# Seven products for eight over the whole contraction, in the up-projection of a one-core decoder layer

## The chip, the cores and the metric

The kernel runs on one core of one Trainium2 chip. The metric is the device time of one launch in microseconds. Three runs of the kernel before took 2917.29, 2924.40 and 2925.81 us; their median is 2924.4.

## The reference

One decoder layer for 2048 prompt rows and 64 sample rows of width 1024: a mixer of two recurrent parts (RWKV-7 and HGRN2), then two post-norms around a squared-ReLU MLP. The change is in the MLP part alone:

```
h1 = layer_norm(ALPHA * h + mix, ln1_g, ln1_b)
up = square(relu(h1 @ w_up))                # 1024 -> 4096
ff = up @ w_down                            # 4096 -> 1024
h  = layer_norm(ALPHA * h1 + ff, ln2_g, ln2_b)
```

All is float32. The kernel splits each operand of a product into a high part and a low part (the difference) and takes three matmuls for one: high by high, high by low, low by high (`mm3`). So one 128-column step of a contraction is three matmuls.

## The kernel before

**Stages.** The mixer's instructions are ordered by a planner (`Sched`), which also plans the first rows of the MLP (`begin`, `enter`). From `rest` on (about 1430 us) the order is written out: each engine takes its instructions in the order in which the program emits them, and so does SyncE, which issues the transfers. The MLP goes through three blocks of rows: block 0 with 576 rows (`first`), blocks 1 and 2 with 768 each (`block`). TensorE is PE, weight loads PEld, VectorE DVE, ScalarE ACT, GpSimd POOL, SyncE SP.

**A unit of blocks 1 and 2.** `up(j)` makes two column tiles of `up`, j and j + 16, for 768 rows, which stand as two halves of 384. `down` then adds the products of the two tiles before with the rows of `w_down` to the accumulators `acc`: twelve steps of six matmuls with 512 columns, each in one of four banks, followed by an add on DVE. With the two column tiles, the two row halves and two halves of the contraction, a product of 2 x 2 by 2 x 2 parts can be made with seven products instead of eight, if sums of the operands are formed first (Strassen's scheme in Winograd's form). Before, this is done over the first half of the contraction (four of eight tiles of 128; `seven`, two tiles each); over the other half all four products are made directly (`direct`, four tiles each). The seven products go to four banks; copies and adds on ACT and DVE (`m1`, `m5`, `u2` in the tile `mt`) combine them. `done` makes relu, square and a high part on ACT and a low part on DVE, into `uh` and `ul`.

**Operands of a unit.** `w_up` comes as `raw` tiles of 1024 columns; sums are formed on DVE (`t12`, `t34`), and `split` makes high and low parts (ACT, then DVE) into four slots of 512 columns, `uph` and `upl`. Some slots are filled twice a unit, the second time within `up` (`s3`, `s4`). The rows of `w_down` are split as whole 1024-column tiles into a ring of three (`wdh`, `wdl`).

**Between blocks.** `enters` transposes the next block's rows (PE), forms their sums (`sums`) and splits them into `xo`, `xd` and `xs`. Its nine entries are taken one by one within the last two `down` passes. The finished block's norms (`layer_norm`: statistics, center, scale) are put into `later` step by step in the last pass; `step` takes one from there. `finish` is the last down-projection of block 2, four tiles at once.

Of the kernel before, what the change touches and what calls it, by code (L numbers as in the profile page):

```python
# [8 lines left out]
F32 = mybir.dt.float32  # L9
# [40 lines left out]
STEPS = 8  # L50
# [1623 lines left out]
def mlp_phase(ctx, tc, em, a, o, z, banks, sch):  # L1674
# [16 lines left out]
    def bank(nm):  # L1691
        b0, n = {"pd": (0, 4), "pu": (4, 4), "pt": (4, 4)}[nm]
        i = cnt.get(nm, 0)
        cnt[nm] = i + 1
        return fix["banks"][b0 + i % n]
# [8 lines left out]
    def begin(free):  # L1704
# [7 lines left out]
        lnp.extend(pool.tile([128, 1024], F32, name=f"lnp{i}") for i in range(4))  # L1712
        for i in range(4):
            src = a["lnp"][i:i + 1, :]
            em.dma(lnp[i], bass.AP(tensor=src.tensor, offset=src.offset, ap=[[0, 128], [1, 1024]]))
            yield now() + APART
# [3 lines left out]

        for x in "hl":
            fix["xd" + x] = pool.tile([128, 3072], F32R, name="xd" + x)
            fix["xo" + x] = pool.tile([128, 2304], F32R, name="xo" + x)
        slots.extend((pool.tile([128, 512], F32R, name=f"uph{i}"), pool.tile([128, 512], F32R, name=f"upl{i}")) for i in range(4))
        yield "go"
        for mi, (t0, mt) in enumerate(blocks[0]):
# [5 lines left out]
            if mi == 0:  # L1732
                ahead(1, 0)
                yield now() + APART
                ahead(2, 0)
                yield now() + APART
            sch.add(enter(mi, mt, sch.clk[SP] + DMA_TIME + 3000), 2)
            yield "go"
        ahead(2, 1)
        yield "go"  # L1740

    def enter(mi, mt, t):

        yield t
        for f in layer_norm(accs[0][mi], mt, 0):
            f()
            yield
        for g in range(2):
            ps = yield from PT.get()
            tr_in(0, mi, g, ps)  # L1750
            yield
            tr_out(0, mi, g, ps)
            PT.put(ps)
            yield "go"


    slots = []
    uses = []
    for f in range(0, NFT, 2):
        uses.append([("up", f, 2 * (f % 2))])  # L1760
        if f == NFT - 2:
            uses.append([("up", f + 1, 2)])
        if f:
            uses.append([("wd", f - 2, None), ("wd", f - 1, None)])
        if f < NFT - 2:
            uses.append([("up", f + 1, 2)])
    uses.append([("wd", NFT - 2, None), ("wd", NFT - 1, 2)])
    w = {"dma": 0, "split": 0, "use": 0}
    raws, splits = [], []

    def ahead(n_dma, n_split):
        while w["split"] < min(n_split, len(uses)):
            while w["dma"] <= w["split"]:
                fetch()
            u = uses[w["split"]]
            splits.append([halves(raw, at) for (_, f, at), raw in zip(u, raws.pop(0))])
            w["split"] += 1
        while w["dma"] < min(n_dma, len(uses)):
            fetch()

    def halves(raw, at=None):

        if at is not None:
            for i in range(2):
                split(slots[at + i], raw[:, 512 * i:512 * i + 512])
            return slots[at:at + 2]
        h = ring("wdh", 3, [128, 1024], F32R)
        l = ring("wdl", 3, [128, 1024], F32R)
        split((h, l), raw)
        return [(h[:, 512 * i:512 * i + 512], l[:, 512 * i:512 * i + 512]) for i in range(2)]  # L1790

    def split(hl, x):
        em.act(hl[0], x, AF.Copy)
        em.tt(hl[1], x, hl[0].bitcast(F32), OP.subtract)

    def fetch():
        raws.append([load(nm, f) for nm, f, _ in uses[w["dma"]]])
        w["dma"] += 1
# [6 lines left out]
    def use():  # L1805

        ahead(0, w["use"] + 1)
        w["use"] += 1
        return splits.pop(0)

    def prepare():

        ahead(w["use"] + 2, w["use"] + 1)
# [12 lines left out]
    def layer_norm(t, mt, gi, then=None):  # L1826
# [520 lines left out]
```

## Time and profile before

| | us |
|---|---|
| median of three runs | 2924.4 |
| the profiled execution | 2921.14 |
| its span, first to last instruction | 2919.4 |
| PE busy | 2837.4 (97%) |
| DVE busy | 1972.7 (68%) |
| ACT busy | 1158.8 (40%) |
| POOL busy | 432.1 (15%) |

Matmuls overlap: each is shown from its start to the end of its pipeline, so the time that one takes is read from the starts of two that follow one another. A timeline row gives the start, the duration, the engine, the line and the operation with the tiles it writes and reads; in brackets stands how long the engine was idle before it and who released it. Where several equal instructions follow each other, one row shows them with their count and the time from the first start to the last end. L97 is the line of the matmul helper, L112 that of ACT's, L156 that of the two-input operation on DVE or POOL.

### The profile page before, as it was taken

Reading aid. Unit: us, or ns where it says so; the run is one execution under the profiler, and the core shown is the slowest. Engines: PE = TensorE matmul, PEld = TensorE weight load, DVE = VectorE, ACT = ScalarE, POOL = GpSimd, SP = SyncE. Lnnn points to the kernel's source line nnn. Section 1 sums busy time; section 2 is a strip of 40 time slices with the busy share of each in tenths; the row PEclk is TensorE's granted clock in tenths of the full one; section 3 lists DMA queues with packets and bytes.
Section 4 is the critical chain, followed back from the end, with each engine's and each line's share of the span. In section 5 each row is a group of like instructions: output and inputs, shape, how many; then the busy total and the mean of one; then the engine's idle time right before and its main releaser. Section 6 shows DMA issues by size and latency. Waiting matters only on the chain.

```text
span 2919.4 us, 54442 instructions
## 1 busy us (share of the span) xinstructions
PE 2837.4 (97%) x22110; PEld 2480.9 (85%) x22110; DVE 1972.7 (68%) x3826; ACT 1158.8 (40%) x2465; POOL 432.1 (15%) x430
## 2 busy tenths in 40 slices
PE   8999999999999999899999999899999999999998
PEld 8988877778777777889988889799999989999997
DVE  5776757868687687854445664776677677666566
ACT  5455323443444335333333333443443344433442
POOL 4332111011110012335300010200000020000002
PEclk9999999999999999999999999999999999999999
DMA  7535444534353443448532222122121112211221
GB/s 272 194 104 199 153 132 138 172 103 141 103 160 116 124 131 120 135 133 276 183 104 98 85 80 85 61 87 105 59 84 61 58 66 73 102 64 58 72 74 58
DMA packets 173196, 337.32 MB, mean 116 GB/s; under 512 B 29712, under 2 KB 51472, under 8 KB 172944
## 3 DMA queue, kind: packets, MB, share of 16 engines
q1 hardware_dynamic: 172944, 333.83, 34.3%
q8 instruction: 173, 2.83, 0.4%
q14 instruction: 79, 0.65, 0.1%
HBM read 270.65 MB, written 63.11 MB: 114 GB/s over the span
## 4 chain that ended last, share of the span: by engine, by line
PE 80%; DVE 12%; ACT 3%; DMA 2%; issue 2%; POOL 1%; SPq 0%; POOLq 0%; DVEq 0%; ACTq 0%
PE bank L97 79%; PE bank L108 2%; DVE rhsb L156 1%; DVE xt L156 1%; DVE xt L1005 1%; DVE et L160 1%; DMA raww<-in_wout 1%; DVE rs L160 1%; DVE et L900 1%; DVE acc L156 1%; POOL wl L156 0%; DVE st L1848 0%; DVE bk L160 0%; DVE upl L156 0%; DVE xl L156 0%
## 5 line engine op out<-in xcount | busy, mean ns | idle before, releaser
L156 DVE TENSOR_TENSOR acc<-bank,acc 128x512 f32<-128x512 f32 (+1 forms) x532 | 358.7, 686 | 119.2 <-PE bank L97 117.5
L97 PE MATMUL bank<-wdh,uh 128*128 128x512 f32 (+1 forms) x1054 | 413.3, 392 | 6.7 <-DVE acc L156 5.1
L97 PE MATMUL bank<-wdl,uh 128*128 128x512 f32 (+1 forms) x1054 | 411.9, 391 | 0.8 <-DVE wdl L156 0.8
L97 PE MATMUL bank<-wdh,ul 128*128 128x512 f32 (+1 forms) x1054 | 411.8, 391 | 0.0
L97 PE MATMUL bank<-xh,wh 128*128 128x512 f32 (+1 forms) x1040 | 383.9, 369 | 10.9 <-ACT wh L112 7.8
L97 PE MATMUL bank<-xl,wh 128*128 128x512 f32 (+1 forms) x1040 | 380.2, 366 | 0.6 <-DVE xl L156 0.6
L97 PE MATMUL bank<-xh,wl 128*128 128x512 f32 (+1 forms) x1040 | 374.8, 367 | 0.9 <-POOL wl L156 0.8
L97 PE MATMUL bank<-wh,xh 128*128 128x256 f32 (+1 forms) x816 | 248.8, 305 | 8.5 <-DVE rs L160 8.5
L97 PE MATMUL bank<-xdh,upl 128*128 128x384 f32 (+1 forms) x768 | 247.8, 323 | 5.6 <-DVE upl L156 5.6
L97 PE MATMUL bank<-xdh,uph 128*128 128x384 f32 (+1 forms) x768 | 247.2, 322 | 0.0
L97 PE MATMUL bank<-xdl,uph 128*128 128x384 f32 (+1 forms) x768 | 247.2, 322 | 0.0
L97 PEld LDWEIGHTS bank<-wdh,uh 128*128 128x128 f32 (+1 forms) x1054 | 194.8, 185 | 51.3 <-DVE acc L156 6.0
L97 PE MATMUL bank<-wh,xl 128*128 128x256 f32 (+1 forms) x816 | 235.0, 288 | 3.0 <-POOL xl L156 3.0
L97 PE MATMUL bank<-wl,xh 128*128 128x256 f32 (+1 forms) x816 | 235.1, 288 | 1.8 <-POOL wl L156 1.8
L156 DVE TENSOR_TENSOR upl<-raw,uph 128x512 fp32r<-128x512 f32 (+1 forms) x262 | 161.4, 628 | 110.4 <-ACT uph L112 110.2
L97 PEld LDWEIGHTS bank<-wdh,ul 128*128 128x128 f32 (+1 forms) x1054 | 194.9, 185 | 45.4
L97 PEld LDWEIGHTS bank<-xh,wh 128*128 128x128 f32 x1040 | 197.6, 190 | 40.8 <-ACT wh L112 8.0
L97 PEld LDWEIGHTS bank<-wdl,uh 128*128 128x128 f32 (+1 forms) x1054 | 194.9, 185 | 43.9 <-DVE wdl L156 1.1
L97 PEld LDWEIGHTS bank<-xl,wh 128*128 128x128 f32 x1040 | 197.5, 190 | 29.5 <-issue 4.8
L97 PEld LDWEIGHTS bank<-xh,wl 128*128 128x128 f32 x1040 | 196.1, 190 | 29.1 <-issue 4.8
L112 ACT ACTIVATE uph<-raw 128x512 fp32r<-128x512 f32 (+1 forms) x262 | 141.6, 569 | 169.0 <-DVE raw L156 144.8
L156 POOL TENSOR_TENSOR wl<-raww,wh 128x512 fp32r<-128x512 f32 x120 | 161.6, 1352 | 278.6 <-ACT wh L112 246.7
(261 smaller groups left out, 5843.8 us busy)
## 6 DMA issues: line engine op xcount, KB each, us to landing
raw<-in_wup SPq DMA_DIRECT2D x96, 512.0 KB, 3.5
raw<-in_wdown SPq DMA_DIRECT2D x96, 512.0 KB, 3.5
wh<-h_w SPq DMA_DIRECT2D x156, 256.0 KB, 2.7
wl<-l_w SPq DMA_DIRECT2D x156, 256.0 KB, 2.9
raww<-in_wout SPq DMA_DIRECT2D x64, 256.0 KB, 3.0
raww<-in_win SPq DMA_DIRECT2D x52, 256.0 KB, 3.3
h_w<-wh SPq DMA_DIRECT2D x52, 256.0 KB, 2.8
l_w<-wl SPq DMA_DIRECT2D x52, 256.0 KB, 2.3
```

The lines of the kernel that those rows point to most:

```text
L97: self.nc.tensor.matmul(out, lhsT, rhs, start=start, stop=stop, skip_group_check=skip)
L108: self.nc.tensor.transpose(out, in_, ident)
L112: self.nc.scalar.activation(out, in_, func, **kw)
L156: (self.nc.vector if eng == DVE else self.nc.gpsimd).tensor_tensor(out, a, b, op=op)
L160: self.nc.vector.scalar_tensor_tensor(out, a, s, b, op0=op0, op1=op1)
L900: nc.vector.tensor_tensor_scan(L[:, c0:c0 + per], ones.to_broadcast([128, per]), sg[:, c0:c0 + per], 0.0, op0=OP.add, op1=OP.add)
L1005: nc.vector.transpose(out, in_)
```

## The change

`up(j)` makes seven products over the whole contraction, with four tiles of 128 each, and no direct ones. For this `enters` forms all sums over eight tiles (`rows`, then `sums`, which has its low parts of sums made by POOL), with twelve entries; the operands stand in `xo` and `xs` alone. The sums of `w_up` are over 512 columns (`one` to `seven`), two of the subtractions on POOL; seven operand slots are filled per unit, three of them within `up`. `up` takes three banks of the four in turn. The weights of `w_down` are split in half tiles of 512 into four fixed slots (`wslots`); `down` goes through all rows with the first half of the columns and then with the second. A block's last norms are appended to `later` after its last `down` pass, so that they run behind the next block's operands, in `up` and `down` of its first units; `down` takes a norm step at its steps 0, 4 and 8 (before at step 0 alone). Only two norm parameter rows are held, and loaded anew when the kind of norm changes (`norm_params`).

Of the functions in the diff below the added and the kept lines are shown; the removed ones stand in the kernel above.

```diff
+    def load_down(*fs):
+        for f in fs:
+            new["wd", f] = load("wd", f)
+
+    def split(hl, x, eng=DVE):
+        em.act(hl[0], x, AF.Copy)
+        em.tt(hl[1], x, hl[0].bitcast(F32), OP.subtract, eng=eng)
+
+    def split_up(f):
+        raw = new.pop(("up", f))
+        for i in range(2):
+            split(slots[2 * (f % 2) + i], raw[:, 512 * i:512 * i + 512])
+
+    def split_down(fs, hfs=(0, 1)):
+        for hf in hfs:
+            for i, f in enumerate(fs):
+                split(wslots[2 * hf + i], new["wd", f][:, 512 * hf:512 * hf + 512])
+
+    def norm_params(gi, i):
+        src = a["lnp"][2 * gi + i:2 * gi + i + 1, :]
+        em.dma(lnp[i], bass.AP(tensor=src.tensor, offset=src.offset, ap=[[0, 128], [1, 1024]]))
...
+            got = []
+
+            def rows(g, mi=mi, got=got):
+                for m in (mi, mi + 3):
+                    got.append(bank("pu"))
+                    tr_in(bi, m, g, got[-1])
+
+            def sums(mi=mi, got=got):
+                a11, a21, a12, a22 = got
+                cs = slice(mi * 128, mi * 128 + 128)
+                t1, t2, t3 = (fix["mt"][:, 512 * i:512 * i + 512] for i in range(3))
+
+                def put(nm, k0, x, eng=DVE):
+                    part(nm, k0, 384, cs, x.rearrange("p (k t) -> p k t", k=4), eng)
+
+                em.act(t3, a21, AF.Copy)
+                em.tt(t1, a22, t3, OP.add)
+                put("xs", 0, t1, POOL)
+                em.tt(t2, t1, a11, OP.subtract)
+                put("xs", 4, t2, POOL)
+                em.tt(t3, a11, t3, OP.subtract)
+                put("xs", 8, t3, POOL)
+                put("xo", 0, a11)
+                em.tt(t1, a12, t2, OP.subtract)
+                put("xs", 12, t1, POOL)
+                put("xo", 8, a22)
+                put("xo", 4, a12)
+
+            def scale(mi=mi):
+                for m in (mi, mi + 3):
+                    t = accs[bi % 2][m]
+                    em.act(t, t, AF.Copy, scale=ALPHA)
+
+            out += [lambda r=rows: r(0), lambda r=rows: r(1), sums, scale]
...
+    def down(bi, fs, tasks, last=False, todo=()):
 
         acc = accs[bi % 2]
+        n = 0
+        for hf in range(2):
+            for mi, (t0, mt) in enumerate(blocks[bi]):
                 ps = bank("pd")
+                partial(ps, mi, mt, fs, wslots[2 * hf:2 * hf + 2], True, True)
                 s = slice(512 * hf, 512 * hf + 512)
                 em.tt(acc[mi][0:mt, s], ps[0:mt], acc[mi][0:mt, s], OP.add)
+                if todo and n % 2 == 0:
                     todo.pop(0)()
+                for x in tasks.get(n, ()):
+                    x()
+                if n % 4 == 0 and not todo:
+                    step()
+                n += 1
         if last:
             while todo:
                 todo.pop(0)()
+            lns = []
+            for mi, (t0, mt) in enumerate(blocks[bi]):
+                def put(t0=t0, mt=mt, t=acc[mi]):
+                    em.dma(o["y"][t0:t0 + mt], t[0:mt])
+
+                lns.append(layer_norm(acc[mi], mt, put))
+            for i in range(len(lns) + 2):
                 for j in range(3):
+                    if 0 <= i - j < len(lns):
...
+    def last_two(bi, fs, gs):
+
+        todo = enters(bi + 1)
+        n = len(blocks[bi])
+        down(bi, fs, {n + 1: [lambda: split_down(gs, (0,))]}, todo=todo)
+        down(bi, gs, {0: [lambda: split_down(gs, (1,))], 2: [unit.one], 4: [unit.two], 6: [unit.three], 8: [unit.four]}, last=True, todo=todo)
...
+        def one(self):
             self.f, self.g = self.new
             split(slots[0], self.f[:, 0:512])
+            em.tt(self.f[:, 0:512], self.g[:, 0:512], self.f[:, 0:512], OP.subtract)
+
+        def two(self):
+            f, g = self.f, self.g
+            split(slots[1], f[:, 0:512])
+            em.tt(f[:, 0:512], g[:, 512:1024], f[:, 0:512], OP.subtract)
+            em.tt(g[:, 0:512], g[:, 512:1024], g[:, 0:512], OP.subtract, eng=POOL)
+
+        def three(self):
+            split(slots[2], self.f[:, 0:512])
+
+        def four(self):
+            split(slots[3], self.g[:, 512:1024])
+
+        def five(self):
+            split(slots[0], self.g[:, 0:512])
+
+        def six(self):
+            split(slots[1], self.f[:, 512:1024])
+            em.tt(self.f[:, 512:1024], self.f[:, 512:1024], self.f[:, 0:512], OP.subtract, eng=POOL)
+
+        def seven(self):
             split(slots[2], self.f[:, 512:1024])
...
+            y, x, d = (bank("pu")[:, 0:384] for _ in range(3))
+            m1, m5, u2 = (fix["mt"][:, 512 * i:512 * i + 384] for i in range(3))
+
+            def seven(ps, nm, k0, slot, first=False):
                 wh, wl = slots[slot]
                 for k in range(4):
                     ws = slice(128 * k, 128 * k + 128)
-                    mm3(ps, wh[:, ws], wl[:, ws], *xs("xd", k, t, 768), first and k == 0, last and k == 3, True)
+                    xs = [fix[nm + z].rearrange("p (k t) -> p k t", t=384)[:, k0 + k] for z in "hl"]
+                    mm3(ps, wh[:, ws], wl[:, ws], *xs, first and k == 0, k == 3, True)
 
...
+            seven(y, "xo", 0, 0, True)
             em.act(m1, y, AF.Copy)
+            unit.five()
+            seven(x, "xs", 0, 1, True)
             em.act(m5, x, AF.Copy)
+            unit.six()
             step()
+            seven(y, "xs", 4, 2)
             em.act(u2, y, AF.Copy)
+            unit.seven()
+            if j:
+                split_down((j - 1, j + 15), (0, 1) if j == 15 else (0,))
+            if j == 15:
+                load_down(f, g)
+            seven(x, "xs", 12, 3)
+            em.tt(u2, x, u2, OP.add)
             if j < 15:
                 unit.load()
+            done(u2, g, 0)
+            seven(y, "xs", 8, 0)
             em.tt(m5, y, m5, OP.add)
+            if 0 < j < 15:
+                split_down((j - 1, j + 15), (1,))
+            if j < 15:
+                load_down(f, g)
             if j == 15 and not end:
                 unit.load()
+            if not j:
+                unit.one()
+                unit.four()
+            done(m5, g, 384)
+            seven(d, "xo", 4, 1, True)
+            em.tt(m1, d, m1, OP.add)
+            if not j:
+                unit.two()
+            done(m1, f, 0)
+            if j == 15 and end:
+                late(3, f, 0)
+                late(0, f, 1)
+                late(1, g, 0)
+            seven(y, "xo", 8, 2)
+            if j == 15 and end:
+                late(2, g, 1)
+            if not j:
+                unit.three()
             c = ring("c", 2, [128, 384], F32)
             em.act(c, y, AF.Relu)
             squared(c, f, 384)
...
+                down(bi, (j - 1, j + 15), {2: [unit.one], 4: [unit.two], 6: [unit.three], 8: [unit.four]})
...
                     step(len(later))
+                    for i in range(2):
+                        norm_params(0, i)
                     next_rows(bi + 1)
...
         step(len(later))
...
+        if not end:
+            for i in range(2):
+                norm_params(1, i)
+            last_two(bi, (14, 30), (15, 31))
             return
...
+        ws = [wslots[0::2], wslots[1::2], [slots[3], slots[0]], [slots[1], slots[2]]]
+        finish(bi, (14, 30, 15, 31), ws)
```

## Rows read from the trace of the kernel before

**Rows 1.** The page: busy time, share of the span and instructions of each engine.

```profile
PE 2837.4 (97%) x22110; PEld 2480.9 (85%) x22110; DVE 1972.7 (68%) x3826; ACT 1158.8 (40%) x2465; POOL 432.1 (15%) x430
```

**Rows 2.** Windows (busy us per engine, PE's granted clock, DMA): block 0, block 1.

```profile
1500.00:1550.00 50.00, 50.00 (x293) 43.90 (x292) 24.70 (x38) 17.02 (x34) 0.00 (x0) 1.00 0.39 139
...
1905.00:2340.00 435.00, 435.00 (x2198) 396.20 (x2197) 291.75 (x489) 170.53 (x322) 5.53 (x14) 1.00 0.21 75
```

**Rows 3.** Timeline (start, duration, engine, operation) of PE, one unit of block 2.

```profile
2499.72 0.39 PE L97 MATMUL bank<-wdh,uh 128*128 128x512 f32 x1
...
2504.94 0.39 PE L97 MATMUL bank<-wdh,ul 128*128 128x512 f32 x1
...
2508.32 0.33 PE L97 MATMUL bank<-xdh,uph 128*128 128x384 f32 x1
...
2510.23 0.33 PE L97 MATMUL bank<-xdh,upl 128*128 128x384 f32 x1
```

**Rows 4.** Timeline of ACT in that unit; in brackets the idle time before.

```profile
2508.39 0.63 ACT L112 ACTIVATE uph<-raw 128x512 fp32r<-128x512 f32 x1 [0.43 <-PE bank L97]
...
2511.66 0.49 ACT L112 ACTIVATE mt<-bank 128x384 f32<-128x384 f32 x1 [2.63 <-PE bank L97]
2512.05 0.41 ACT L112 ACTIVATE uph<-raw 128x256 fp32r<-128x256 f32 x1
2512.35 1.07 ACT L112 ACTIVATE mt<-mt 128x384 f32<-128x384 f32 x2
2513.46 0.53 ACT L112 ACTIVATE uh<-mt 128x384 fp32r<-128x384 f32 x1
...
2522.77 1.14 ACT L112 ACTIVATE uph<-raw 128x512 fp32r<-128x512 f32 x2
```

**Rows 5.** Timeline of DVE in that unit.

```profile
2509.06 0.69 DVE L156 TENSOR_TENSOR upl<-raw,uph 128x512 fp32r<-128x512 f32 x1 [1.81 <-ACT uph L112]
...
2514.02 0.56 DVE L156 TENSOR_TENSOR ul<-mt,uh 128x384 fp32r<-128x384 f32 x1 [1.10 <-ACT uh L112]
...
2523.38 1.28 DVE L160 SCALAR_TENSOR_TENSOR acc<-acc,rsd,lnp 128x1024 f32<-128x1024 f32 x1
2524.57 1.28 DVE L156 TENSOR_TENSOR acc<-bank,acc 128x512 f32<-128x512 f32 x2
```

**Rows 6.** Groups by line and form of POOL: count, busy us, mean ns, idle time before.

```profile
L156 POOL TENSOR_TENSOR wl<-raww,wh 128x512 fp32r<-128x512 f32 x120 | 161.6, 1352 | 278.6 <-ACT wh L112 246.7 <-PE bank L97 14.0 <-DMA z<-rs 8.1
```

**Rows 7.** Timeline of POOL and of DVE near the end of the mixer.

```profile
1303.63 1.28 POOL L156 TENSOR_TENSOR wl<-raww,wh 128x512 fp32r<-128x512 f32 x1 [1.31 <-ACT wh L112]
...
1344.84 1.97 POOL L156 TENSOR_TENSOR wl<-raww,wh 128x512 fp32r<-128x512 f32 x1 [1.25 <-ACT wh L112]
...
1344.38 1.28 DVE L160 SCALAR_TENSOR_TENSOR acc<-acc,mv,lnp 128x1024 f32<-128x1024 f32 x1
```

**Rows 8.** PE's waits (us in total, times, longest) at the two block changes and the end.

```profile
PE bank L97 <- DVE acc L156: 2.3, 2, 1.4
...
PE bank L97 <- DVE upl L156: 4.1, 1, 4.1
PE bank L97 <- ACT uph L112: 0.7, 1, 0.7
...
PE bank L97 <- DVE acc L156: 2.9, 3, 1.1
PE bank L97 <- DVE upl L156: 1.5, 1, 1.5
...
PE bank L97 <- ACT wdh L112: 1.4, 1, 1.4
PE bank L97 <- DVE wdl L156: 0.8, 1, 0.8
```

**Rows 9.** Timeline of PE after its 4.1 us wait.

```profile
1867.26 0.52 PE L97 MATMUL bank<-xdh,uph 128*128 128x384 f32 x1
...
1871.42 0.52 PE L97 MATMUL bank<-xsl,uph 128*128 128x384 f32 x1
```

More of the change, by code (lines that the diff above doesn't have):

```diff
@@ L1751, in enter @@
             yield
-            tr_out(0, mi, g, ps)
+            part("xo", 4 * g, 576, slice(n, n + mt), ps.rearrange("p (k t) -> p k t", k=4)[:, :, 0:mt])
             PT.put(ps)
+            if g:
+                em.ts(tl[0:mt], tl[0:mt], ALPHA, None, OP.mult, eng=POOL)
             yield "go"
[L1757 to L1798, printed above, removed]
+    new, slots, wslots = {}, [], []
     def load(nm, f):
@@ L2015, in up, with next_up, even, odd @@
                 squared(c, f, c0)
-        todo = []
-        for f in range(0, NFT - 2, 2):
-            up(f)
+        def next_up(f):
+            new["up", f] = load("up", f)
+        def even(f):
             if f:
-                down(0, (f - 2, f - 1), use(), {2: [prepare]})
-            up(f + 1)
+                split_down((f - 2, f - 1))
+            else:
+                split_up(1)
+            if f == NFT - 2:
+                split_up(f + 1)
+                load_down(f, f + 1)
+                return
+            next_up(f + 2)
+            if not f:
+                load_down(0, 1)
+        def odd(f):
+            if f == NFT - 1:
+                unit.load()
+                return
+            split_up(f + 1)
+            next_up(f + 2)
+        for f in range(0, NFT, 2):
+            up(f, lambda: even(f))
+            if 0 < f < NFT - 2:
+                down(0, (f - 2, f - 1), {2: [lambda: split_up(f + 1), lambda: load_down(f, f + 1)]})
+            up(f + 1, lambda: odd(f + 1))
             if f == 8:
@@ L2132, in up @@
-            seven(y, "xs", 2, 1, 256)
+            seven(y, "xs", 4, 2)
             em.act(u2, y, AF.Copy)
-            unit.s4()
+            unit.seven()
[5 more added lines that the diff above has]
+            em.tt(u2, x, u2, OP.add)
             if j < 15:
                 unit.load()
-            done(m1, f, 0)
-            direct(e, 384, 3, first=True)
@@ L2139, in up @@
-            seven(y, "xs", 4, 0, 0)
+            done(u2, g, 0)
+            seven(y, "xs", 8, 0)
             em.tt(m5, y, m5, OP.add)
-            if j:
-                split_down(j - 1, 0)
-            em.tt(m5, e, m5, OP.add)
-            done(m5, g, 384)
-            seven(x, "xs", 6, 0, 256, last=False)
-            if j == 0:
-                unit.s1()
-                unit.t12()
-            direct(x, 0, 3)
-            em.tt(u2, x, u2, OP.add)
-            if j:
-                split_down(j - 1, 1)
```

216 lines of the change are left out of this document (41 added, 175 removed).

## The prediction

> **What bounds the kernel now.** The page's first part shows TensorE (PE) busy 97% of the span, VectorE (DVE) 68%, ScalarE (ACT) 40%, GpSimd (POOL) 15% [rows 1]. Then the stretches: in the middle of block 1 PE is busy for 435.00 of 435.00 us at full granted clock [rows 2], and the list of PE's waits there is empty. So a matmul removed there is time removed, as long as nothing else becomes late. Third, the timeline of one unit (one pass of `up` and one of `down`), engine by engine, because it has the durations and the order [rows 3 to 5]. Last, PE's waits at the block changes, the only places of the MLP where it waits: 2.3 us, 4.1 and 0.7 at the first, 2.9, 1.5 and again 0.7 at the second, 2.2 before the last down-projection [rows 8].
>
> **The matmuls removed.** A unit of blocks 1 and 2 makes two column tiles for 768 rows. Before: seven products over four contraction tiles (7 x 4 x 3 = 84 at full contraction, here half: 42) and four direct ones over the other four (4 x 4 x 3 = 48), 90 matmuls of 384 columns; after: 84. There are 2 x 16 units, so 192 go. Twelve such matmuls start in 2508.32 to 2510.23, 0.174 us apart, though each is shown as 0.33 long because they overlap [rows 3]; the pitch is the price: **-33.4 us**. The 72 matmuls of `down` stay (0.227 apart [rows 3]).
>
> **The chain inside a unit.** All that hid before now has a shorter unit and another order, so I laid the emitted order of `up` on the durations of the rows, us from the unit's first matmul. The method, tried on the old unit, gives its starts within 0.15 us, for instance the ACT chain at 2512.35 and the low part at 2514.06 (trace: 2512.35 and 2514.02 [rows 4, 5]). Durations: an ACT split of 512 columns 0.62, the next 0.52 later; a chain relu, square, copy 1.64; a DVE low part 0.69, the next 0.60 later; a 384-column DVE add 0.56, 0.47 [rows 4, 5]; a hand-over 0.04 (ACT ends 2509.02, DVE starts 2509.06). POOL's 512-column subtraction 1.29 [rows 7] (1.35 on average [rows 6]).
> Each product is 12 matmuls, 2.09 us; its result is there 0.16 after the next has begun.
> - 4.38: ACT copies the second product; 4.77 to 5.39 `six` splits; 5.43 to 6.12 DVE's low part; then `six` subtracts on POOL, 6.21 to 7.50.
> - `seven` splits what POOL wrote, and ACT stands in line for it: 7.53 to 8.15. Behind it come two splits of `split_down`, to 9.19. DVE's three low parts start at 8.19, 8.79, 9.39.
> - The add that makes u2 needs a product finished at 8.52, but is queued behind those on DVE: 9.99 to 10.55. ACT's three steps 10.59 to 12.23. DVE's low part of u2 at 12.26, and only then m5's add, 12.73 to 13.29, though its product was there at 10.61.
> - The seventh product writes the bank `y` that this add reads. PE could start it at 12.53 and waits until 13.34: **0.8 us**.
> Nothing gives it back: the next unit begins later by as much. It holds for passes 1 to 14 of both blocks, 28 x 0.8 = 22.4. In pass 15 all four splits stand ahead of u2's add (1.2 more): 2 x 2.0 = 4.0. In pass 1, which follows pass 0 with no `down` between, the second product takes the bank that pass 0's last relu still reads: 2 x 1.0 = 1.9. Together **+28.3**. Bounds: if ACT's `seven` did not have to wait for POOL, u2's add would start 0.65 earlier and the wait fall to 0.15 (8 us in all); with POOL at its mean 1.35 it is 0.05 longer a unit (30).
>
> **The norms on top.** After m5's add the four chains follow one another, ACT and DVE in turn: m1's add 15.5, the last relu 17.6, its low part 19.3, DVE free at 19.76. The first add of `down` then ends at 20.45; PE needs its bank for step 4 at 20.86. Slack 0.4; the old unit had a norm step ahead of its first add (2523.38, 2524.57 [rows 5]) and PE waited nowhere. A norm step at the end of `up` (center or scale 1.19 of DVE's time [rows 5], the statistics taken as the same) makes PE wait 0.85, the one at step 0 delays the next add and adds 0.45: 1.3 in 12 units (passes 1 to 3 of both blocks, where the norms of the block before now are, and 7 to 12 of block 1), 15.8; a third norm step at step 8 adds 0.8 in five of these, 4.1; small delays in passes 1 and 2 make 1.6. **+21.5**, between 0 (if the slack is 1.3 larger) and 27.
>
> **The block changes.** DVE no longer does norms there (they stood in the last `down` pass), but one call of `sums` holds it for 7 us: seven operations of 0.6, and waits for ACT's copies in between. Four banks cover four steps of `down` (5.4) plus transposes (0.9 each eight), so steps that come after a `sums` wait. The splits of `split_down` and `one` to `four` are queued behind it. Laid out in the same way: change 0 to 1: 2.2, 1.0 and 3.5 within the two passes; 5.0 at the end, because ten pops do not hold the twelve entries: the last `sums` runs when no `down` is left, and the first product needs its low part (three adds 1.8, two ACT copies 1.2, a low part 0.7, an add before, and DVE's backlog); 0.4 later: 12.1. After the old wait of 4.1 PE ran 15 matmuls at 0.32 apart instead of 0.174 (1.2 instead of 2.4 GHz) [rows 9], 2.2 us; I add the same here, 14.3 against 9.3 (7.1 and 2.2). Change 1 to 2: 2.2, 3.4, 1.3, 0.9 = 7.8 against 5.1. **+7.7**; between -5 (the norms' absence frees DVE entirely) and +12 (half clock after the 3.4 and 3.5 too).
> A rule bears on it: by the Trainium skill, SBUF — State Buffer, section "SBUF: two separate sides", VectorE and GpSimd exclude each other for a whole instruction, on VectorE's side among others when both its inputs lie in SBUF. The trace agrees: a POOL subtraction that starts at 1344.84 within DVE's center (1344.38 to 1345.66) takes 1.97 instead of 1.29 [rows 7]. By the rule the 24 POOL low parts of the two changes spare DVE, whose operations in `sums` read a bank; were every DVE operation held, the sum would rise by up to 24 x 1.29 = 31 us.
>
> **The rest.** The final four-part down-projection gets its weights in four quarter splits into slots that are free; by the same layout PE waits 1.4 there against 2.2: **-0.8**. Block 0: same matmuls, its weights split at the same places, 0, covered by PE's own work: busy 50.00 us of 50 where DVE is busy 24.70 [rows 2]. If it were gone, a split late by 0.6 would cost 15 x 0.6 = 9. Half-width loops, slots instead of a ring: 0. Reloading the norm parameters: six transfers on SP, each behind norms that are long done, with at least half an `up` until the next weights are issued: 0; if one held the queue, the nearest row is the worst wait for weights, 4.1 [rows 8]. The end of the mixer is planned anew, since `begin` issues two transfers less: 0, from -5 to +5.
>
> **Sum.** -33.4 + 28.3 + 21.5 + 7.7 - 0.8 = +23.3. The profiled execution took 2921.14 (span 2919.4 and 1.7 around), 3.3 below the median of the three runs, within their spread: 2921.1 + 23.3 = **2944 us**, some 0.7 to 0.8% slower. Own range: 2934 to 2962.
>
> **Rivals.**
> - *The saving comes through*: PE reaches the seventh product without a wait. Decides: m5's add must end 0.8 us earlier. For it: DVE is idle for half of `up`, and PE waited nowhere in the old units. Against it: the order in each queue is fixed, and the layout met the old unit to 0.15 us. Time with no unit waits: 2921 - 33.4 + 7.7 - 0.8 = 2895. With an easier block change too, 2885. This is the other side.
> - *About even*: the unit wait shrinks because POOL's result comes earlier or a hand-over costs less; then the slack before the norms grows by 0.65 too. Waits of 8 + 2 x 1 and some 12 of the norms: 2921 - 33.4 + 22 + 7 + 4 = 2920.
> - *The clock*: half clock after each unit wait, 2.2 x 28 = 62 more: 3006. Against it: old waits of 1.4 and less were followed by matmuls at full pitch.
> - *Products not fewer*: excluded by the loops, which give 84.
>
> **Chances.** Forecast 0.66, saving comes through 0.15, even 0.16, clock or another late transfer 0.03. A difference below 0.3% (9 us) can't be told from none in these runs: faster 0.17 (the first rival, and a corner of the second), same 0.15, slower 0.68. Range 2907 to 2967: it leaves out most of the first rival and the clock.
>
> **What would show it.** PE's matmuls less by 192, and in passes 1 to 14 one wait of 0.7 to 0.9 us before the product on `xo` tiles 8 to 11, released by DVE's add on `mt`; ACT idle until POOL's `raw` subtraction just before; in passes 7 to 12 of block 1 waits at steps 4 and 5 of `down`, released by DVE's `acc`; a wait near 5 us at the start of block 1. Wrong if block 1's middle still shows PE without waits, or if POOL's subtraction ends before ACT comes to it.

## The result and the profile after

The changed kernel takes 2948.7 us (median of 4 runs, 2945.15 to 2953.42), the kernel before beside it 2923.85 (4 runs, 2917.29 to 2925.81): ratio 1.009, 95% interval 1.0069 to 1.0111. It is slower, by 25 us where 23 were forecast. The profiled execution took 2953.42 (span 2951.3); that is the longest of the four.

The page's first line after, against [rows 1]: 192 matmuls fewer and 12.4 us less of PE's busy time, and yet a longer span.

```profile
PE 2825.0 (96%) x21918; PEld 2448.9 (83%) x21918; DVE 1985.0 (67%) x3812; ACT 1208.6 (41%) x2576; POOL 511.9 (17%) x505
```

PE's waits from the last unit of block 0 to the end (us in total, times, longest; L108 in such rows is the line of the transposes); before, such rows stood at the block changes and the end alone [rows 8]:

```profile
PE bank L97 <- DVE mt L156: 27.8, 30, 1.9
PE bank L97 <- DVE acc L156: 18.9, 23, 3.2
PE bank L97 <- DVE xol L156: 5.1, 2, 4.6
PE bank L97 <- ACT c L112: 3.7, 2, 1.9
...
PE bank L97 <- DVE upl L156: 0.5, 2, 0.2
```

The first row is the seventh product's wait, once in each of passes 1 to 15 of both blocks. One unit of block 2 after, PE (first matmul of the unit, the seventh product of it, first matmul of the next):

```profile
2603.02 0.34 PE L97 MATMUL bank<-xoh,uph 128*128 128x384 f32 x1
...
2616.53 0.41 PE L97 MATMUL bank<-xoh,uph 128*128 128x384 f32 x1 [0.69 <-DVE mt L156]
...
2635.09 0.34 PE L97 MATMUL bank<-xoh,uph 128*128 128x384 f32 x1
```

The unit takes 2635.09 - 2603.02 = 32.07 us. The same two rows before:

```profile
2505.17 0.34 PE L97 MATMUL bank<-xoh,uph 128*128 128x384 f32 x1
...
2537.24 0.34 PE L97 MATMUL bank<-xoh,uph 128*128 128x384 f32 x1
```

Again 32.07: six matmuls are gone from each unit, and the whole of it is waited away (that the two are equal to the last digit is chance). The chain that does it, after, in time: POOL's subtraction, ACT's split of what it wrote, ACT's next split, DVE's low parts, u2's add, u2's low part, m5's add.

```profile
2609.30 1.30 POOL L156 TENSOR_TENSOR raw<-raw 128x512 f32<-128x512 f32 x1 [13.94 <-issue]
2610.63 0.63 ACT L112 ACTIVATE uph<-raw 128x512 fp32r<-128x512 f32 x1 [0.59 <-POOL raw L156]
2611.29 0.69 DVE L156 TENSOR_TENSOR upl<-raw,uph 128x512 fp32r<-128x512 f32 x1 [2.13 <-ACT uph L112]
2611.90 1.29 DVE L156 TENSOR_TENSOR wdl<-raw,wdh 128x512 fp32r<-128x512 f32 x2
2613.11 0.55 DVE L156 TENSOR_TENSOR mt<-bank,mt 128x384 f32<-128x384 f32 x1
2615.36 0.56 DVE L156 TENSOR_TENSOR ul<-mt,uh 128x384 fp32r<-128x384 f32 x1 [1.71 <-ACT uh L112]
2615.84 0.55 DVE L156 TENSOR_TENSOR mt<-bank,mt 128x384 f32<-128x384 f32 x1
```

The seventh product starts 0.14 after the last row's end. DVE sits idle for 1.71 us, with m5's add next in its queue but one: its product was long there, and the low part of u2 in front of it waits for ACT.

At the change from block 0 to 1 (before: 1.4 at the most, then 4.1 in the first `up` [rows 8]), three rows with PE's waits; the 384-column matmuls behind the third run at half clock, 0.32 apart as in [rows 9]:

```profile
1839.83 0.44 PE L97 MATMUL bank<-wdh,uh 128*64 128x512 f32 x1 [1.91 <-DVE acc L156]
1857.56 0.80 PE L97 MATMUL bank<-wdh,uh 128*128 128x512 f32 x1 [3.23 <-DVE acc L156]
1868.87 0.69 PE L97 MATMUL bank<-xoh,uph 128*128 128x384 f32 x1 [4.57 <-DVE xol L156]
```

**One measure for all that follows.** Executions of one kernel differ by some us in the mixer, ahead of everything that the experiments touch. So beside the medians I use the *tail*: from the first matmul of block 0's last unit to the end of the span. Before that is 2919.4 - 1804.06 = 1115.3, after 2951.3 - 1803.71 = 1147.6:

```profile
1804.06 0.29 PE L97 MATMUL bank<-xdh,uph 128*128 128x288 f32 x1
```

```profile
1803.71 0.29 PE L97 MATMUL bank<-xoh,uph 128*128 128x288 f32 x1
```

Kernels that differ only ahead of it repeat it within 0.8 (the last two of the table). The ratios are taken over single executions, without one of the kernel before that ran in a slower state (3439.6 us), so they are not quite the quotients of the two medians.

| kernel | median | before, same chip | ratio, 95% interval | tail |
|---|---|---|---|---|
| before | | | | 1115.3 |
| changed | 2948.7 | 2923.85 | 1.0090 (1.0069 to 1.0111) | 1147.6 |
| splits late | 2928.97 | 2920.01 | 1.0033 (1.0020 to 1.0046) | 1125.5 |
| `six` on DVE | 2931.53 | 2920.01 | 1.0040 (1.0027 to 1.0053) | 1128.8 |
| norm steps moved | 2926.45 | 2920.01 | 1.0026 (1.0017 to 1.0036) | 1125.1 |
| before, norms behind | 2910.98 | 2920.01 | 0.9967 (0.9956 to 0.9978) | 1103.2 |
| both moves | 2897.62 | 2919.71 | 0.9926 (0.9913 to 0.9938) | 1098.4 |
| four banks in turn | 2906.36 | 2919.71 | 0.9953 (0.9939 to 0.9966) | 1106.4 |
| that, sums in two | 2895.74 | 2919.71 | 0.9921 (0.9908 to 0.9935) | 1095.4 |
| banks by parity | 2894.53 | 2918.43 | 0.9908 (0.9891 to 0.9924) | 1094.6 |
| parity, sums in two | 2885.02 | 2918.43 | 0.9881 (0.9867 to 0.9896) | 1084.1 |
| changed, four loads | 2951.79 | 2920.68 | 1.0106 (1.0091 to 1.0122) | 1147.3 |
| before, two loads | 2913.90 | 2920.68 | 0.9978 (0.9969 to 0.9987) | 1114.5 |

### The profile page after: what moved, and what is told of

Its sections match the earlier page's. It is cut to its first block, busy times and chain, and to the rows that moved or that the text cites. A ratio compares the mean times of both kernels' runs of the same rounds, so it can differ in the third digit from the quotient of the medians.

```text
span 2951.3 us, 54436 instructions
## 1 busy us (share of the span) xinstructions
PE 2825.0 (96%) x21918; PEld 2448.9 (83%) x21918; DVE 1985.0 (67%) x3812; ACT 1208.6 (41%) x2576; POOL 511.9 (17%) x505
## 4 chain that ended last, share of the span: by engine, by line
PE 59%; DVE 18%; issue 11%; ACT 8%; POOL 2%; DMA 2%; SPq 0%; DVEq 0%; POOLq 0%; ACTq 0%
PE bank L97 57%; ACT mt L112 2%; DVE rhsb L156 2%; DVE xt L156 2%; DVE mt L156 2%; POOL raw L156 2%; PE bank L108 2%; DVE wdl L156 1%; DVE xt L1005 1%; ACT uh L112 1%; DVE acc L160 1%; DVE ul L156 1%; ACT uph L112 1%; DVE acc L156 1%; DVE upl L156 1%
## 5 line engine op out<-in xcount | busy, mean ns | idle before, releaser
L97 PE MATMUL bank<-wdh,uh 128*128 128x512 f32 (+1 forms) x1064 | 421.1, 396 | 20.2 <-DVE acc L156 18.9
L156 DVE TENSOR_TENSOR acc<-bank,acc 128x512 f32<-128x512 f32 (+1 forms) x532 | 351.5, 684 | 102.9 <-PE bank L97 100.0
L97 PE MATMUL bank<-xoh,uph 128*128 128x288 f32 (+1 forms) x896 | 283.0, 316 | 32.9 <-DVE mt L156 27.8
L156 DVE TENSOR_TENSOR upl<-raw,uph 128x512 fp32r<-128x512 f32 x292 | 201.4, 699 | 162.2 <-ACT uph L112 162.1
L97 PE MATMUL bank<-xoh,upl 128*128 128x288 f32 (+1 forms) x896 | 280.4, 313 | 0.0
L97 PE MATMUL bank<-xol,uph 128*128 128x288 f32 (+1 forms) x896 | 280.2, 313 | 0.0
L112 ACT ACTIVATE uph<-raw 128x512 fp32r<-128x512 f32 x292 | 174.4, 623 | 205.7 <-DVE raw L156 182.4
L156 POOL TENSOR_TENSOR raw<-raw 128x512 f32<-128x512 f32 x64 | 89.2, 1394 | 784.6 <-DVE raw L156 410.9
```

Of the source, the lines that this page charges most:

```text
L97: self.nc.tensor.matmul(out, lhsT, rhs, start=start, stop=stop, skip_group_check=skip)
L112: self.nc.scalar.activation(out, in_, func, **kw)
L156: (self.nc.vector if eng == DVE else self.nc.gpsimd).tensor_tensor(out, a, b, op=op)
```

## The experiments

Theory: the saved products are lost in two sorts of waits in the units, on m5's add (DVE's queue behind POOL's result) and on the adds of `down` (norm steps on DVE), and a rest at the block changes. Rivals: a transfer, the clock, or an engine that is simply full.

**Splits late.** All four splits of `split_down` behind m5's add, instead of two ahead of u2's.

```
-            if j:
-                split_down((j - 1, j + 15), (0, 1) if j == 15 else (0,))
...
-            if 0 < j < 15:
-                split_down((j - 1, j + 15), (1,))
+            if j:
+                split_down((j - 1, j + 15))
```

> The changed kernel, with split_down moved: in up, all four splits of w_down's tiles are emitted behind m5's add instead of two ahead of u2's add. My theory (the queue order on DVE and ACT makes the wait before the seventh product): u2's add starts about 1.2 us earlier, the waits of 0.7 on DVE mt go in passes 1 to 14, and so do the two of 1.9 in pass 15; the end of up gets later on DVE, so the waits on acc at steps 4 and 5 grow with norm steps. Sum of my layout: 51.3 us of waits become 33.3; 2931 us. Rival (the bank y is the cause, or POOL alone): the wait before the seventh product stays at 0.7 in each pass, and the time at 2945 or more.

```profile
PE bank L97 <- DVE acc L156: 27.4, 23, 3.2
...
PE bank L97 <- DVE mt L156: 2.9, 6, 0.7
```

22.1 us less of the tail. The wait on m5's add falls from 27.8 to 2.9, but that on `acc` rises from 18.9 to 27.4: DVE's work is now nearer to `down`, where the norm steps are. A unit without norms takes 31.20 us, one with norms still 32.8 (33.1 in the changed kernel).

**`six` on DVE.** The subtraction of `six` runs on DVE, not on POOL.

```
-            em.tt(self.f[:, 512:1024], self.f[:, 512:1024], self.f[:, 0:512], OP.subtract, eng=POOL)
+            em.tt(self.f[:, 512:1024], self.f[:, 512:1024], self.f[:, 0:512], OP.subtract)
```

> The changed kernel, with the subtraction of six on DVE (0.69 us) instead of POOL (1.30 us and a hand-over of 0.09). My theory (both the stand of ACT for POOL and the splits ahead of u2's add make the wait): the wait before the seventh product falls from 0.7 to 0.2 or less, and because the end of up comes earlier, the acc waits shrink too; 12 us less in my layout, 2936 us. Rival (only the order of split_down counts): no change, 2949. Rival (POOL alone): no wait before the seventh product at all in any pass, pass 15 included.

```profile
PE bank L97 <- DVE mt L156: 9.3, 15, 1.3
```

18.8 us of tail. In the units without norms the wait is all but gone (they take 31.4 us), though DVE has more to do: there it was ACT standing in line for POOL's result, and not a lack of room on DVE. In the six units of block 1 with norms a wait of 0.6 stays and nothing is gained (33.1 us, as in the changed kernel); pass 15, with four splits ahead of the add, keeps 1.3.

**Norm steps moved.** None at the end of `up`; those of `down` at its products 5, 7, 9 and 10.

```
-                if n % 4 == 0 and not todo:
+                if n in (5, 7, 9, 10) and not todo:
                     step()
...
             squared(c, f, 384)
-            step()
```

> The changed kernel without the norm step at the end of up, and with down's norm steps at its steps 5, 7, 9 and 10 instead of 0, 4 and 8. My theory (a norm step ahead of the first adds makes PE wait for their banks): the acc waits within the blocks (7.0 and 3.6 us idle) go, the mt waits of 0.7 stay; 21 us less, 2927 us. Rival (DVE has too much work in those units, wherever the norm steps lie): acc waits come back at later steps of down, 2940 or more.

```profile
PE bank L97 <- DVE mt L156: 24.9, 29, 1.9
PE bank L97 <- DVE acc L156: 10.2, 4, 3.2
```

22.5 us of tail, though the rows show only 11.6 us less of idle time: the four waits that are left on `acc` are those of the block changes. A wait row counts from the end of the matmul before, which is 0.16 behind the moment at which the next could have started, and small delays leave no row at all. Over units it is plain: with norms 33.1 before the move, 32.0 after it.

**Before, norms behind.** The kernel before, with a block's last norms moved behind the loop of the last `down`, as the change does; nothing else.

```
-            if last:
-                def put(t0=t0, mt=mt, t=acc[mi]):
...
         if last:
             while todo:
                 todo.pop(0)()
+            for mi, (t0, mt) in enumerate(blocks[bi]):
+                def put(t0=t0, mt=mt, t=acc[mi]):
...
```

> The kernel before with one part of the change alone: a block's last norms are appended behind its last down pass and run in the next block's first units (norm parameters stay resident, norm steps where they were). My theory: DVE is freed of about 7 us at each block change, the wait of 4.1 us for upl and the half-clock matmuls behind it (2.2) go, and some of the acc waits; in the next units the old order has room for the steps; 2916 us, 8 less. Rival (norms cost the same wherever they are): waits of the same sum in passes 1 to 4, 2924. Rival (the norms behind are what made the changed kernel slower): 2930 or more.

PE's waits at its change from block 0 to 1, all that are left:

```profile
PE bank L97 <- DVE acc L156: 1.4, 1, 1.4
PE bank L97 <- ACT uph L112: 0.7, 1, 0.7
```

The 4.1 us wait of [rows 8] and the half clock of [rows 9] are gone; 12.1 us of tail, where 8 were expected. So this part of the change is a gain by itself, and what else is new at the block changes (the list of `enters` above all, but the half-tile splits too) loses all of it and more.

**Both moves.** The splits of the first half tiles (hf 0) behind m5's add, those of the second (hf 1) and the load at `down`'s first product, and the norm steps as above.

```
...
-                down(bi, (j - 1, j + 15), {2: [unit.one], 4: [unit.two], 6: [unit.three], 8: [unit.four]})
+                def second(j=j):
+                    split_down((j - 1, j + 15), (1,))
+                    load_down(j, j + 16)
+
+                down(bi, (j - 1, j + 15), {0: [second], 2: [unit.one], 4: [unit.two], 6: [unit.three], 8: [unit.four]})
```

> The changed kernel with both moves at once: the splits of the first half tiles (hf 0) behind m5's sum, those of the second half tiles (hf 1) and the load at the first product of down, and a norm's steps at products 5, 7, 9 and 10 of down, none at the end of up. Theory: what the changed kernel lost are two sorts of waits of PE, 27.8 us on m5's sum (30 of them) and about 22 us on acc (the sum of down, delayed by a split or a norm step). Each move alone gave 20 and 22 us back, and the splits moved alone raised the acc waits from 18.9 to 27.4 us; with both moves both sorts go, 43 to 50 us in all: 2899 to 2906 us, about 18 us under the kernel before. mt waits below 3 us, acc waits about 10 us (the four at the block changes alone). Rival: ACT, DVE and POOL are simply full in a unit of 32 us, and a piece moved out of one place is late in the next: then the two gains don't add, new waits of 0.3 to 0.7 us come up in the 28 units (on slots or on ul), and the time stays at 2920 or above.

```profile
PE bank L97 <- DVE acc L156: 10.2, 4, 3.2
...
PE bank L97 <- ACT c L112: 3.7, 2, 1.9
PE bank L97 <- DVE mt L156: 1.2, 3, 0.4
```

The gains add (22.1 and 22.5 us alone, 49.2 us of tail together), and the time is 22 us under the kernel before, 1 to 2 us below the range expected. So no engine was full, as the rival would have had it. A unit, by its first matmul and the next one's:

```profile
2587.99 0.34 PE L97 MATMUL bank<-xoh,uph 128*128 128x384 f32 x1
...
2619.09 0.34 PE L97 MATMUL bank<-xoh,uph 128*128 128x384 f32 x1
```

31.10 us, 0.97 less than before: this is what six matmuls are worth when nothing waits.

**Four banks in turn.** Pass 1's second product waits for the bank of pass 0's last (`ACT c`, 1.8 and 1.9); here each pass takes four banks in turn and leaves one out.

```
-            y, x, d = (bank("pu")[:, 0:384] for _ in range(3))
+            y, x, d, _ = (bank("pu")[:, 0:384] for _ in range(4))
```

> The same with four PSUM banks taken in each up instead of three, so that the second product of pass 1 no longer takes the bank that the last product of pass 0 has just filled. Theory: the two waits of pass 1 (1.8 and 1.9 us, one in each block) go, 3 to 4 us less than with both moves alone: 2896 to 2902. Rival: another wait (the slot of that product, or its weights) ends at the same time; then no difference.

```profile
PE bank L97 <- ACT c L112: 7.8, 2, 3.9
```

A miss: 8.0 us slower. With four in turn, every pass begins with the same bank, so pass 1's *first* product takes the bank that pass 0's last has just filled. I had counted the banks and not looked at which one is due.

**Four banks, sums in two.** At the first change the list is cut into ten entries, so that none is left when `down` ends; `sums` takes its half as an argument.

```
...
+                def lead(r=rows, prev=out[-1] if out else None):
+                    if prev is not None:
+                        prev()
+                    r(0)
+                    r(1)
+
+                out[-1:] = [lead, lambda s=sums: s(0), lambda s=sums: s(1), scale]
```

> The same as with four banks, and at the change from block 0 to block 1 the sums of a row pair are cut into two entries of the list that down works off (behind the third of the sums), the scaling goes in front of the next pair's transposes, and the two rows of transposes are one entry, so that all ten entries find a place among the ten products. Theory: the waits at this change (1.9, 3.2 and 4.6 us, the last at the first product of block 1 with half-clock matmuls behind it) come from what is left of the list behind the last product. They fall by about 4 us and the one at the first product is gone with its half clock, about 2 us: 4 to 8 us less than with four banks alone, 2889 to 2897. Rival: the transposes now wait for their banks in the middle of down (pu banks held until the second half of the sums), with 2 us and more at each of the three; then no gain, or a loss of up to 4 us.

11.0 us of tail against four banks alone, more than the 4 to 8 expected, so that it ends 3.0 below both moves in spite of the banks. The time, 2895.7, lies in the range. The transposes that the rival had waiting three times for 2 us and more wait twice for 1.3.

**Banks by parity**, and the same with the sums in two:

```
+            y, x, d = (fix["banks"][4 + i][:, 0:384] for i in ((3, 1, 2) if j % 2 else (0, 1, 2)))
```

> Both moves, with the PSUM banks of up chosen by the pass: an even pass takes banks 0, 1, 2 of the four, an odd one 3, 1, 2. The version that took four in turn (0, 1, 2 in every pass) was 9 us slower than the one with three in turn: its pass 1 put the first product into the bank that pass 0 had just filled, and waited 3.9 us in each block instead of 1.8, with matmuls at half clock behind it. Theory: the wait is on the bank that the last product of the pass before has filled, and nothing else is behind it: by the pass's parity both waits of pass 1 go, and the 1.2 us of the transposes at the second block change with them, 3.7 + 1.2 = 5 us and some half clock: 2889 to 2894, against 2897.6 for three in turn. Rival: the four slots or the weights of these products come no earlier; then the waits stay at 1.8 to 3.9 us under another name, and the time at 2897 or above.

> The same banks by parity, with the list of the change from block 0 to block 1 in ten entries (sums in two, scaling and both rows of transposes in one entry). With four banks in turn this list was worth 10.6 us (2906.4 to 2895.7), 5.0 us of it waits. Theory: the rest was the half clock behind the 4.6 us wait at the first product of block 1, which that list takes away, and it doesn't depend on the banks: again 9 to 11 us less than by parity alone: 2879 to 2884. Rival: half of it was the half clock behind the two waits one behind the other (4.6, then 3.9 in pass 1), of which the second is gone by parity; then 5 to 7 us, 2884 to 2888.

Parity alone, at the first change, then parity with the sums in two:

```profile
PE bank L97 <- DVE acc L156: 5.2, 2, 3.2
PE bank L97 <- DVE xol L156: 4.6, 1, 4.6
PE bank L97 <- ACT mt L112: 1.2, 1, 1.2
```

```profile
PE bank L97 <- DVE acc L156: 2.6, 1, 2.6
PE bank L108 <- DVE xol L156: 2.6, 2, 1.3
PE bank L97 <- ACT mt L112: 1.1, 1, 1.1
```

Parity gives 3.8 us against both moves, not 5: `ACT c` is gone, but in each block 1.2 to 1.3 us of a wait on `mt` stand in its place, as the rival said in part. The sums in two give 10.5 more, the 9 to 11 expected, and it can be counted. (The time alone, 2885.0, lies 1 us above the range expected and in the rival's; the tail decides.) From block 0's last unit to pass 2 of block 1, 8.8 us: 4.7 of waits; 384-column matmuls at half clock 8 instead of 17, at 0.15 each 1.4; `down`'s 512-column ones at half clock (0.43 apart instead of 0.227) 2 instead of 15, at 0.2 each 2.6. The other 1.7 lie at the second change, where 7 of `down`'s matmuls run at half clock instead of 14; the list there is the same in both kernels, so this part is not the list's doing. With four banks in turn the list gave 9.5 us at the first change in the same way, 4.6 of it waits and about 5 clock. This last version is the fastest: 2885.0 us, 1.2% under the kernel before.

**The transfers in `begin`.** The tail is 32.3 us longer after the change, the medians differ by 25. (In the two profiled executions the MLP begins at the same time, 1428.22 and 1427.87; but the changed kernel's was the longest of its four.) The missing 7 us should then lie in the mixer's end, where `begin` issues two transfers less. The changed kernel with four:

```
-        for i in range(2):
-            norm_params(0, i)
+        for i in range(4):
+            norm_params(0, i % 2)
             yield now() + APART
```

> The changed kernel with four transfers of norm parameters in begin, as the kernel before had them (each is issued twice into the same tile), instead of two; nothing else. In the traces the mixer's last 120 us, from the last product on itk to the MLP's first matmul, are 126.4 and 130.0 us long in the kernel before and in its variant, and 118.0 to 121.9 in the changed kernel and its variants; the MLP alone is 32 us longer in the changed kernel's trace, while the medians differ by 25. Theory: begin leaves a fixed gap of 4 us behind every transfer, so two less bring the first rows and their transposes forward, and the transposes stand between other matmuls than before; the four transfers put this stretch back to 126 us or more, and the time to 2953 to 2957. Rival: the stretch is shorter because of the way in which block 0's operands are written (one pair of tiles instead of two), and the transfers do nothing: 2949, the stretch 118 to 122.

> The kernel before with two transfers of norm parameters in begin; the other two are issued in block 0's MLP, behind the product of f = 8, far ahead of the last norms that use them. Theory of the gaps: the mixer's last stretch falls from 126.4 to 118 to 122 us, the whole time by 4 to 8 us: 2912 to 2916. Rival (the stretch depends on how the operands are written): no difference, 2920.

In the other run the loop of the kernel before goes over two rows instead of four, and the other two transfers are issued in block 0's MLP. The stretch runs from the last product on `itk` to the MLP's first matmul (in the kernel before that is one on `xdh`, not the later one on `xoh` to which the expectation counted; so 124.9 there and 128.5 in its variant, not 126.4 and 130.0). The kernel before with two transfers:

```profile
1299.60 0.27 PE L108 MATMUL bank<-cst,itk 128*128 128x128 f32 x1
...
1419.75 0.29 PE L97 MATMUL bank<-xdh,uph 128*128 128x288 f32 x1
```

120.2 us, and the whole 6.8 us faster than its neighbour, as the gaps would have it; the rival (no difference) is excluded on this side. The changed kernel with four:

```profile
1303.07 0.38 PE L108 MATMUL bank<-cst,itk 128*128 128x128 f32 x2
...
1425.91 0.29 PE L97 MATMUL bank<-xoh,uph 128*128 128x288 f32 x1
```

122.8, against 118 to 121.9 with two, and 31.1 us above the kernel before instead of 24.9. Here the expectation was not met: stretch and time (2951.8) lie between the theory's (126 or more, 2953 to 2957) and the rival's (118 to 122, 2949). The intervals of the two ratios overlap, so in the changed kernel the size stays open.

## Why the prediction was right

**The chain inside a unit** held step by step. Forecast from the unit's first matmul, and measured from 2603.02: POOL's subtraction 6.21 and 6.28; ACT's `seven` 7.53 and 7.61; u2's add 9.99 and 10.09; m5's add 12.73 and 12.82; the seventh product 13.34 and 13.51. The wait was put at 0.8 and costs 32.07 - 31.10 = 0.97. ACT in line for POOL is shown by `six` on DVE (in units without norms), the queue in front of u2's add by the late splits. With both moves 49.2 us are taken out; the sum had 22.4 + 4.0 + 21.5 = 47.9 for the same waits.

**The matmuls removed**: 0.97 a unit, not 1.04, 31.0 in 32 units instead of 33.4. The 0.174 came from twelve matmuls of the old unit. In a unit with both moves the 48 of the second to the fifth product start 0.177 apart on average, the others 0.174: 84 take 14.73 us, where the 90 of the old unit took 15.71.

**The norms on top**: 21.5 forecast, 22.5 by moving them. The price of a unit was off (1.1 where 1.3 was put), the units behind a block change cost more: 3.2 and 1.1 in the two that follow pass 1, where the old block's norms are worked off. Part of that is POOL's (below).

**Pass 1's bank**: 1.9 forecast; the waits were 1.8 and 1.9, 3.7 in all. The last relu was done later than the layout had it; the trace has a reason for it (below).

**The block changes**: +7.7 forecast. With both moves the two stretches from the last unit before a change to pass 2 take 115.6 and 113.6 us, before 110.8 and 109.2. They hold two and three passes of `up`, so 4.9 us of matmuls have gone from them, and the rest has grown by 14.1, some 4 of it pass 1's bank, so about 10. The wait near 5 at the first product was there (4.57, forecast 5.0), and 1.91 and 3.23 for 2.2 and 3.5; the 1.0 between them did not show. The half clock did more than I put there, in the changed kernel not only behind the 4.57, but seven matmuls of `down` behind each of the other two, ten of `up` behind the 1.82 of pass 1, and seven of `down` at the second change: 21 x 0.2 + 26 x 0.15 = 8.1 us, where the kernel before had 2.2 [rows 9]. It was in the upper bound and not in the value. The term is also a difference of two larger ones that I had not taken apart: the norms' move gives 12 (measured in the kernel before), so the rest of what is new there costs about 22. That was not measured as a whole; cutting the first list anew gave some 9 of it back.

**POOL and DVE.** The low parts on POOL were not held by DVE: the 24 of them took 1289 ns on average beside DVE operations that read a bank, like the undisturbed 1.28 of [rows 7].

```profile
L156 POOL TENSOR_TENSOR xsl<-mt,xsh 128x512 fp32r<-128x512 f32 x24 | 30.4, 1289 | 154.7 <-ACT xsh L112 154.7
```

So the 31 us that stood at the other end are excluded. The rule in the Trainium skill, SBUF — State Buffer, section "SBUF: two separate sides", by which VectorE and GpSimd exclude each other among others when both inputs of VectorE's operation lie in SBUF, agrees with this row: these had one in a bank.

But the prediction asked this of the 24 low parts alone. POOL's 64 subtractions of `two` and `six` run beside DVE operations whose inputs both lie in SBUF, and eight of the 64 took 1.67 to 2.27 us instead of 1.30. In pass 4 of block 2 a norm step on DVE starts just before the subtraction of `six`, and the seventh product waits 1.61 instead of 0.69:

```profile
2544.06 1.28 DVE L160 SCALAR_TENSOR_TENSOR acc<-acc,rsd,lnp 128x1024 f32<-128x1024 f32 x1
2544.23 2.27 POOL L156 TENSOR_TENSOR raw<-raw 128x512 f32<-128x512 f32 x1 [13.57 <-DVE upl L156]
2552.43 0.41 PE L97 MATMUL bank<-xoh,uph 128*128 128x384 f32 x1 [1.61 <-DVE mt L156]
```

With both moves three subtractions of `six` still took 2.27, one in pass 3 of block 1 and two in passes 3 and 4 of block 2; the three waits of 0.4 that are left on m5's add stand in these units, and they take 31.8 to 32.1 us, where every other one of passes 2 to 14 takes 31.10. It goes the other way round, too. In pass 0 a low part on DVE that starts while POOL subtracts (1884.97 to 1886.65) takes 1.65 instead of 0.56:

```profile
1885.41 1.65 DVE L156 TENSOR_TENSOR ul<-mt,uh 128x384 fp32r<-128x384 f32 x1
```

The add behind it, ACT's chain and the relu that pass 1's bank waits for come later by as much, in both blocks: about what the wait there was longer than forecast. This is read from the traces; no run moved these operations apart.

**The rest**: the last down-projection waits 0.5 us, not 1.4; from its stretch (58.1 us with both moves, 61.4 before, 0.97 off for the matmuls) the finish is 2.3 better, not 0.8. Half clock is in this as well: behind the waits of 1.4 and 0.8 [rows 8] eight matmuls of the kernel before ran 0.43 apart, 1.6 us in all, and after the change none does. This stretch of the kernel before (PE busy, granted clock, DMA):

```profile
2878.70:2882.20 3.50, 3.50 (x10) 0.51 0.00 0
```

And the step that I put at 0, the end of the mixer, is the one that missed most: two transfers less bring the MLP forward by some 7 us (6.8 in the kernel before, measured alone). The gap behind each transfer stands in the code, and I named its bounds (-5 to +5) without working it through.

So the total is nearer than its parts: in the tail the change costs 32.3 us where the terms gave 23.3 (matmuls 2.4 more, the unit and norm waits 1.3, pass 1 about 2, the changes about 2.5, finish -1.5, and 2.5 in the three units with a long subtraction on POOL, for which there was no term), and the mixer's end pays most of that back. The mechanism in the units was right; that the total came within 5 us of the forecast is in part luck.

**The rivals.** The saving comes through once the waits are gone, and by the place that the prediction named as decisive (m5's add), but not in the changed kernel. The clock did not fall in the units: in the changed kernel the granted clock is 1.00 from 2440 to the last unit's end, and half-clock matmuls stand at the block changes alone. But the reason given against this rival, that old waits of 1.4 and less were followed by full pitch, did not hold before the last down-projection (above). A transfer ended none of these waits: the rows from block 0's last unit on name DVE and ACT alone.

## What to carry to other kernels

When matmuls are taken out of a loop in which PE never waits, lay the other engines' queues out in order over the shorter loop before counting the gain: here an add whose input was ready stood for 2 us behind work that waited for another engine, and moving splits and norm steps by half a unit was worth 49 us where the matmuls were worth 31. When a helper engine takes over work, look at every operation that will run beside it, not only at the new ones. Take a term that is a difference of two edits apart and size each; and count the fixed gaps in the emitted order, of a transfer that is dropped too.

## What was not expected of the hardware

In the changed kernel five waits at the block changes (1.82, 1.91, 3.13, 3.23 and 4.57 us) were followed by 7 to 17 matmuls at half clock, 1.4 to 2.6 us on top of the wait. In the units, waits of 0.7 once in 32 us were not, and neither were those of 1.6 behind the changes or of 1.9 in pass 15. The length of the wait does not decide it alone: three other waits of 1.86 to 1.93 us at the second change were not followed by half clock either. The same wait there, first with banks by parity (half clock: 0.43 apart), then with the sums in two as well (full clock: 0.23 apart):

```profile
2351.54 0.50 PE L97 MATMUL bank<-wdh,uh 128*128 128x512 f32 x1 [1.93 <-DVE acc L156]
...
2352.62 0.63 PE L97 MATMUL bank<-wdh,uh 128*128 128x512 f32 x1
2353.05 0.63 PE L97 MATMUL bank<-wdl,uh 128*128 128x512 f32 x1
```

```profile
2342.42 0.50 PE L97 MATMUL bank<-wdh,uh 128*128 128x512 f32 x1 [1.93 <-DVE acc L156]
...
2343.22 0.40 PE L97 MATMUL bank<-wdh,uh 128*128 128x512 f32 x1
2343.45 0.39 PE L97 MATMUL bank<-wdl,uh 128*128 128x512 f32 x1
```

What decides stays open here; tails of two kernels can differ by 1 to 2 us at each such wait for this alone.

And the idle time in the wait rows understates what a wait costs, here by 0.28 us: 0.69 shown, 0.97 between the units' starts.
